# Hybrid block on one core: the low part of half of every second MLP weight tile made by an adding DMA, and 56 instead of 44 of the 128 pairs of K tiles by seven products

## The chip, the cores and the metric

The kernel runs on one core of one Trainium2 chip. The number that counts is the device time of one execution in microseconds, here the median of three runs. TensorE (PE in the profile) multiplies, VectorE (DVE), ScalarE (ACT) and GpSimd (POOL) work on tiles in the on-chip memory SBUF, PSUM holds the sums of TensorE, and SyncE (SP) issues most of the DMAs.

## The reference

One layer of a hybrid trunk on 256 tokens, width 2048, in float32. The change lies in the last third, the squared-ReLU MLP:

```python
D_MODEL = 2048; SEQ = 256; D_FF = 4 * D_MODEL
...
def squared_relu_mlp(n, w1, w2):
    return jnp.square(jax.nn.relu(n @ w1)) @ w2
...
    n = rms_norm(h, norm_mix_w[layer])
    h = h + hybrid_token_mixer(n, ...)      # input projection, two head groups, output projection
    n = rms_norm(h, norm_ffn_w[layer])
    h = h + squared_relu_mlp(n, w_ff1[layer], w_ff2[layer])
return rms_norm(h, norm_final_w)
```

`w_ff1` is 2048 x 8192 and `w_ff2` 8192 x 2048, so each is read once, as 64 tiles of 128 partitions x 2048 float32 (1 MB).

## The kernel before, in words

**Precision.** TensorE takes each float32 operand as two fp32r numbers: `hi`, the value rounded to fp32r, and `lo`, the rest. For a weight tile ACT makes `hi` by a copy (line 122) and DVE makes `lo = w - hi` (line 123). A product of two blocks is then three matmuls of 128x128 by 128x512: hi by hi, lo of the tokens by hi, hi of the tokens by lo of the weights (lines 925, 926, 927, in `product`).

**Pairs of K tiles.** A weight tile of the MLP holds a 2x2 block of the weight matrix: two blocks of the contraction dimension (a pair of K tiles) by two blocks of 512 columns, in the order B12, B11, B21, B22. The tokens come as a 2x2 block too (two halves of 128 tokens by the same two K tiles). Their product takes eight block products (`plain_quad`, 24 matmuls, summed in the four PSUM banks `E`), or seven with sums of blocks (Winograd's form of Strassen's scheme, `sum_quad`, 21 matmuls). The seven products need differences of the weight blocks, which DVE forms in `TT` (lines 965, 968, 969), and a third and half a fourth pair of hi and lo: `hi4`, `lo4`. They go into the first three banks of `E` and into four more banks `M`, which are joined once per column group (`joins`) and added to `E`.

**Which pairs.** `w_ff1` is worked in eight groups of 1024 columns (`ng`, lines 990 on), each over eight pairs `kp`; `SUMS` says which of them go by seven products: three in the even groups, four in the odd ones, 28 in all. The token operands (with their sums) are made once and stay in `sets` and `sets2`. `w_ff2` is worked in two halves (`q`, line 1105 on) of 32 pairs; `SUMS2` names eight of each 32, 16 in all. Its token operands are made pair by pair, `a2_plain` (one split of 512 columns, `gs`) or `a2_sums` (four sums `S` of 128 columns and splits of 384 and 512, `st`). Together 44 of 128 pairs go by seven products.

**Buffers.** Three buffers hold weight tiles (`wpool`). The pairs of hi and lo of 1024 columns go to five places in turn: three in `spool` (`hi`, `lo`) and two in `wp2` (`hi2`, `lo2`), in `split_pair`. `hi4`, `lo4`, `TT`, `S` and `st` have one place each.

**Order.** The program is written tile by tile, and a scheduler then sets the order on each engine; engines work in that order, and an instruction waits on its engine until what it needs is there and the place it writes is free. SP issues the loads of the weight tiles (lines 1000 and 1107), each once one of the three places is free. Between two groups of `w_ff1` the four finished outputs pass through ACT (relu), are transposed on PE (line 937) and squared by ACT (`turn`, line 939, held back in `fills`). POOL has no work in the MLP but two instructions at its end.

Of the kernel before, what the change touches and what calls it, by code (L numbers as in the profile page):

```python
# [75 lines left out]
def hybrid_block(ctx: ExitStack, tc: tile.TileContext, x, xt, w_in, w_ab, params, w_out, w_ff1, w_ff2,  # L76
# [747 lines left out]

    KP = KT // 2
    SUMS = ((2, 4, 6), (1, 2, 4, 6))
    WITH_SUMS = (2, 1, 4, 6)
    sets = bpool.tile([P, 8192], F32R, tag="xT", name="sets")  # L830
    sets2 = tp.tile([P, 3 * 1792], F32R, tag="s2", name="sets2")
    plain = [kp for kp in range(KP) if kp not in SUMS[0]]
# [4 lines left out]

    def a_sums(kp):
        n = WITH_SUMS.index(kp)
        t, at = (sets2, (n - 1) * 1792) if n else (sets, 6144)  # L840
        return t[:, at:at + 1792].rearrange("p (s n t) -> p s n t", s=2, n=7)

    h = hpool.tile([P, 2 * D], F32, tag="h", name="h").rearrange("p (f c) -> p f c", f=2)
# [68 lines left out]
    NF = DFF // P  # L912
    NG = NF // 2
    NGR = 8
    gt = []

    def g(kp):
# [33 lines left out]
            if (n, kk) == (3, 0):  # L951
                fill(n_fill)

    def plain_weights(w):
        B12, B11 = halves(split_pair(w[:, 0:1024]))
        B21, B22 = halves(split_pair(w[:, 1024:2048]))
        return (B11, B12), (B21, B22)

    def sum_quad(E, M, A, w, a0, z0):

        TT = tq.tile([P, 2048], F32, tag="TT", name="TT")
        B = [w[:, c * 512:(c + 1) * 512] for c in range(4)]
        T1, T2, T4 = [TT[:, c * 512:(c + 1) * 512] for c in (0, 2, 3)]
        B21, B22 = halves(split_pair(w[:, 1024:2048]))
        DVE.tensor_tensor(out=TT[:, 0:1024].rearrange("p (a c) -> p a c", a=2), in0=view(w, 0, [[1536, 2], [1, 512]]),
                          in1=view(w, 512, [[-512, 2], [1, 512]]), op=ALU.subtract)
        B1, B3 = halves(split_pair(TT[:, 0:1024]))
        DVE.tensor_tensor(out=T2, in0=B[3], in1=T1, op=ALU.subtract)
# [22 lines left out]
    for ng in range(NGR):  # L991


        bank_e, bank_m = (acc_a, acc_b) if ng % 2 == 0 else (acc_b, acc_a)
        E = [bank_e() for _ in range(4)]
        M = None
        with_sums = SUMS[ng % 2]
        for kp in range(KP):
            w = wtile()
            SP.dma_start(w, w_ff1[ng * KP + kp])  # L1000
            if kp not in with_sums:
                st = a_plain(kp)
                plain_quad(E, lambda kk, hf: [st[:, kk, c + hf * P:c + hf * P + P] for c in (0, T)], plain_weights(w),
                           kp == 0, kp == KP - 1, 0 if kp == 0 else 2)
                if kp == 0:
                    fill(4 if 1 in with_sums else 2)
                if ng == 0 and kp == 1:
                    for hf in range(2):
                        DVE.tensor_tensor(out=fs[:, 4 + hf:5 + hf], in0=fs[:, 2 * hf:2 * hf + 1],
                                          in1=fs[:, 2 * hf + 1:2 * hf + 2], op=ALU.add)  # L1010
                    DVE.tensor_scalar(fs[:, 4:6], fs[:, 4:6], 1.0 / D, EPS, ALU.mult, ALU.add)
                    DVE.reciprocal(fs[:, 6:8], fs[:, 4:6])
                    octx.close()
                    yctx.close()
                    fp = ctx.enter_context(tc.tile_pool(name="fp", bufs=1))
                    gt += [fp.tile([P, NG // 2, 4 * P], F32, tag=f"g{i}", name=f"g{i}") for i in range(2)]
                    cp = c1.enter_context(tc.tile_pool(name="cp", bufs=1))
                continue
            if M is None:
                M = [bank_m() for _ in range(4)]  # L1020
            st = a_sums(kp)
            sum_quad(E, M, [(st[:, 0, n, :], st[:, 1, n, :]) for n in range(7)], w, kp == with_sums[0],
                     kp == with_sums[-1])
            if kp == with_sums[-1]:
                C4 = joins(M)

        for at, p in ((0, E[0]), (2, E[1]), (1, E[2]), (3, E[3])):
            DVE.tensor_tensor(out=C4[:, at], in0=p, in1=C4[:, at], op=ALU.add)
            ACT.activation(C4[:, at], C4[:, at], AF.Relu)
            fills.append(lambda ng=ng, at=at, src=C4[:, at], acc=bank_e: turn(ng, at, src, acc))  # L1030
# [42 lines left out]
            DVE.tensor_scalar(h[:, hf, a:b], o[hf][:, a:b], s, None, ALU.mult)  # L1073
        (ACT if eng is ACT else SP).dma_start(out[0, hf * P:(hf + 1) * P, a:b], h[:, hf, a:b])

    SUMS2 = (3, 7, 10, 14, 17, 21, 24, 28)
    TAIL = 2
    KP2 = NF // 2

# [20 lines left out]
    for q in range(2):  # L1100
# [2 lines left out]
        M = None  # L1103
        held = []
        for kp in range(KP2):
            w = wtile()
            SP.dma_start(w, w_ff2[q * KP2 + kp])
            if kp in SUMS2:
                if M is None:
                    M = [bank_m() for _ in range(4)]  # L1110
# [123 lines left out]
```

## Time and profile before

| | |
|---|---|
| median of 3 runs | 1227.92 us (1227.33 to 1228.0) |
| the profiled execution, its own time | 1227.51 us |
| its span | 1225.8 us |
| mean granted TensorE clock | 0.997 |
| MLP in the profile | from 534 us to the end |

The span is what the profiler saw from the first to the last instruction; 1.71 us of the execution's own time lie around it. In the profile's groups a line can be that of a helper: line 123 is every subtraction that makes a `lo`, and the names before and after the arrow say of what.

### The profile page before, as it was taken

Reading aid. Unit: us, or ns where it says so; the run is one execution under the profiler, and the core shown is the slowest. Engines: PE = TensorE matmul, PEld = TensorE weight load, DVE = VectorE, ACT = ScalarE, POOL = GpSimd, SP = SyncE. Lnnn points to the kernel's source line nnn. Section 1 sums busy time; section 2 is a strip of 40 time slices with the busy share of each in tenths; the row PEclk is TensorE's granted clock in tenths of the full one; section 3 lists DMA queues with packets and bytes.
Section 4 is the critical chain, followed back from the end, with each engine's and each line's share of the span. In section 5 each row is a group of like instructions: output and inputs, shape, how many; then the busy total and the mean of one; then the engine's idle time right before and its main releaser. Section 6 shows DMA issues by size and latency. Waiting matters only on the chain.

```text
span 1225.8 us, 18164 instructions
## 1 busy us (share of the span) xinstructions
PE 1214.8 (99%) x6894; PEld 1007.3 (82%) x6894; DVE 1035.7 (84%) x1455; ACT 778.2 (63%) x1150; POOL 113.5 (9%) x165
## 2 busy tenths in 40 slices
PE   9999999999999999999999999999999999999997
PEld 7888888888778888888888888888888888888886
DVE  7878997799977886689889889889998888989887
ACT  7668766677756765565666656566676665656653
POOL 0132432135111110000000000000000000000000
PEclk9999999999999999999999999999999999999998
DMA  9455555555333555656455645654866556556461
GB/s 339 148 172 185 175 178 184 205 173 168 123 115 128 176 173 210 227 180 238 156 187 206 229 148 177 241 202 153 312 223 228 184 186 225 188 191 227 161 230 70
DMA packets 37144, 233.45 MB, mean 190 GB/s; under 512 B 4696, under 2 KB 5728, under 8 KB 10176
## 3 DMA queue, kind: packets, MB, share of 16 engines
q1 hardware_dynamic: 34848, 229.83, 53.5%
q0 software_dynamic: 1632, 1.72, 0.7%
q8 instruction: 54, 0.88, 0.3%
q10 hardware_dynamic: 576, 0.74, 0.2%
q14 instruction: 34, 0.28, 0.1%
HBM read 227.67 MB, written 4.60 MB: 189 GB/s over the span
## 4 chain that ended last, share of the span: by engine, by line
PE 98%; DMA 0%; issue 0%; DVE 0%; ACT 0%; SPq 0%; POOLq 0%; POOL 0%; DVEq 0%
PE acc L369 11%; PE acc L341 10%; PE acc L926 9%; PE acc L927 9%; PE acc L925 9%; PE accb L926 9%; PE accb L925 9%; PE accb L927 9%; PE acc L342 5%; PE acc L896 4%; PE accb L896 4%; PE accv L341 2%; PE accv L342 1%; PE accb L937 1%; PE acc L937 1%; PE pk L465 1%
## 5 line engine op out<-in xcount | busy, mean ns | idle before, releaser
L123 DVE TENSOR_TENSOR lo<-w,hi 128x1024 fp32r<-128x1024 f32 (+1 forms) x422 | 485.6, 1166 | 113.0 <-ACT hi L122 103.6
L122 ACT CAST hi<-w 128x1024 fp32r<-128x1024 f32 (+1 forms) x422 | 413.8, 994 | 233.1 <-PE acc L926 56.9
L341 PE MATMUL acc<-xT,hi 128*128 128x512 f32 x512 | 182.1, 401 | 1.5 <-ACT hi L122 1.5
L122 ACT CAST hi<-TT 128x1024 fp32r<-128x1024 f32 x88 | 92.0, 1052 | 77.5 <-issue 21.7
L342 PE MATMUL acc<-xT,lo 128*128 128x256 f32 x512 | 139.2, 284 | 0.0
L123 DVE TENSOR_TENSOR lo<-TT,hi 128x1024 fp32r<-128x1024 f32 x88 | 106.8, 1221 | 30.2 <-ACT hi L122 27.8
L369 PE MATMUL acc<-hi,xT 128*128 128x512 f32 x384 | 118.0, 395 | 0.0
L341 PEld LDWEIGHTS acc<-xT,hi 128*128 128x128 f32 x512 | 94.3, 188 | 21.1 <-ACT hi L122 2.0
L925 PE MATMUL acc<-hi,sets 128*128 128x512 f32 x260 | 101.4, 391 | 0.0
L926 PE MATMUL acc<-hi,sets 128*128 128x512 f32 x260 | 101.2, 390 | 0.0
L342 PEld LDWEIGHTS acc<-xT,lo 128*128 128x128 f32 x512 | 96.1, 189 | 4.9 <-DVE lo L123 1.2
L927 PE MATMUL acc<-lo,sets 128*128 128x512 f32 x260 | 95.9, 390 | 0.0
L925 PE MATMUL accb<-hi,sets 128*128 128x512 f32 x224 | 88.0, 393 | 0.0
L926 PE MATMUL accb<-hi,sets 128*128 128x512 f32 x224 | 87.3, 390 | 0.0
L369 PEld LDWEIGHTS acc<-hi,xT 128*128 128x128 f32 x384 | 70.4, 188 | 14.6
L927 PE MATMUL accb<-lo,sets 128*128 128x512 f32 x224 | 78.7, 391 | 0.0
L926 PE MATMUL acc<-hi,gs 128*128 128x512 f32 (+1 forms) x200 | 77.0, 385 | 0.0
L925 PE MATMUL acc<-hi,gs 128*128 128x512 f32 (+1 forms) x200 | 76.7, 385 | 0.0
L927 PE MATMUL acc<-lo,gs 128*128 128x512 f32 (+1 forms) x200 | 75.6, 385 | 0.0
L369 PE MATMUL acc<-lo,xT 128*128 128x512 f32 x192 | 73.2, 397 | 0.0
L926 PE MATMUL accb<-hi,gs 128*128 128x512 f32 x188 | 73.1, 389 | 0.0
L925 PE MATMUL accb<-hi,gs 128*128 128x512 f32 x188 | 72.6, 389 | 0.0
(367 smaller groups left out, 2279.2 us busy)
## 6 DMA issues: line engine op xcount, KB each, us to landing
w<-in_w_ff_dram SPq DMA_DIRECT2D x128, 1024.0 KB, 5.0
w<-in_w_in_dram SPq DMA_DIRECT2D x61, 1024.0 KB, 5.0
w<-in_w_out_dram SPq DMA_DIRECT2D x16, 1024.0 KB, 5.0
w<-in_w_in_dram SPq DMA_DIRECT2D x12, 256.0 KB, 5.4
big<-in_xt_dram SPq DMA_DIRECT2D x8, 256.0 KB, 5.8
h<-in_x_dram SPq DMA_DIRECT2D x2, 1024.0 KB, 6.1
scr_h<-h SPq DMA_DIRECT2D x4, 512.0 KB, 7.3
tail<-scr_h SPq DMA_DIRECT2D x2, 1024.0 KB, 8.5
```

The source lines that it names most:

```text
L122: ACT.copy(hi, w)
L123: last_lo[0] = eng.tensor_tensor(out=lo, in0=w, in1=hi.bitcast(F32), op=ALU.subtract)
L341: PE.matmul(accs[g], lhsT=hi[:, kk, g, :], rhs=xT[:, k, :], start=(k == 0), stop=False)
L342: mm = PE.matmul(accs[g][:, T:], lhsT=lo[:, kk, g, :], rhs=xT[:, k, 0:T], start=False, stop=(k == KT - 1))
L369: mm = PE.matmul(accs[hf], lhsT=xT[:, k, a + hf * P:a + hf * P + P], rhs=ww[:, cs], start=(k == 0 and a == 0 and ww is hi), stop=(k == KT ...
L465: PE.matmul(pk0, lhsT=R[:, 1, 0:P], rhs=qk.rearrange("p a t -> p (a t)"), start=True, stop=True)
L896: PE.matmul(accs[2 * hf + c], lhsT=st, rhs=ww[:, c * 512:(c + 1) * 512], start=(k == 0 and a == 0 and ww is hi), stop=(k == 2 * NH - 1 and ...
L925: PE.matmul(dst, lhsT=ah, rhs=bh, start=start, stop=False)
L926: PE.matmul(dst, lhsT=al, rhs=bh, start=False, stop=False)
L927: PE.matmul(dst, lhsT=ah, rhs=bl, start=False, stop=stop)
L937: PE.transpose(pt[:, c * P:(c + 1) * P], src[:, c * P:(c + 1) * P], ident)
```

## The change

In the MLP the tiles are now fetched by `ff_ahead`, which `ff_tile` calls two tiles ahead of the tile that is worked on. Of every second tile (the odd ones of 128) it also makes the low part of the second half (B21 and B22) without DVE: ACT writes the negated half to a new tile `lod` (as fp32r, so it is rounded as `hi` is), and POOL issues a DMA that reads the same half of the weights from HBM again and adds it to `lod`, so that w - hi stands there. `second_half` then makes only `hi` of that half, by ACT. `lod` has two places in `wp2`, 4 KB per partition each; the space that the program keeps for POOL's DMA descriptors is set to 8192 bytes per partition.

`SUMS` now names four pairs in the even groups and five in the odd ones (36 in all), `SUMS2` ten of each 32 (20 in all). Pair 1 is no longer plain in any group and pair 5 is plain in the even ones; the token sets are laid out anew for that, and the first group takes its pairs in the order 0, 3, 1, 5, 2, 4, 6, 7, with the weights laid out to match. From the second group on all four held-back `turn`s come after the first pair.

```diff
+    def ff_ahead(n):
+        while len(ff) <= min(n, 127):
+            i = len(ff)
+            src = w_ff1[i] if i < 64 else w_ff2[i - 64]
+            w, lo = wtile(), None
+            SP.dma_start(w, src)
+            if i % 2:
+                lo = wp2.tile([P, 1024], F32R, tag="lod", name="lod")
+                ACT.activation(lo, w[:, 1024:2048], AF.Copy, scale=-1.0)
+                POOL.dma_start(lo, src[:, 1024:2048], accum_op=ALU.add)
+            ff.append((w, lo))
+
+    def ff_tile(n):
+        ff_ahead(n + 2)
+        t, ff[n] = ff[n], None
+        return t
+
+    def second_half(wl):
+        w, lo = wl
+        if lo is None:
+            return split_pair(w[:, 1024:2048])
+        n = pairs[0] = pairs[0] + 1
+        pool, t = (spool, "") if n % 5 < 3 else (wp2, "2")
+        hi = pool.tile([P, 1024], F32R, tag="hi" + t, name="hi" + t)
+        ACT.copy(hi, w[:, 1024:2048])
+        return hi, lo
...
-    SUMS = ((2, 4, 6), (1, 2, 4, 6))
-    WITH_SUMS = (2, 1, 4, 6)
+    SUMS = ((1, 2, 4, 6), (1, 2, 4, 5, 6))
+    WITH_SUMS = (2, 5, 1, 4, 6)
...
-    def plain_weights(w):
-        B12, B11 = halves(split_pair(w[:, 0:1024]))
-        B21, B22 = halves(split_pair(w[:, 1024:2048]))
+    def plain_weights(wl):
+        B12, B11 = halves(split_pair(wl[0][:, 0:1024]))
+        B21, B22 = halves(second_half(wl))
...
-    def sum_quad(E, M, A, w, a0, z0):
+    def sum_quad(E, M, A, wl, a0, z0):
...
-        B21, B22 = halves(split_pair(w[:, 1024:2048]))
+        B21, B22 = halves(second_half(wl))
...
-        for kp in range(KP):
-            w = wtile()
-            SP.dma_start(w, w_ff1[ng * KP + kp])
+        for pos, kp in enumerate(ORDER[min(ng, 1)]):
+            w = ff_tile(ng * KP + pos)
...
-                           kp == 0, kp == KP - 1, 0 if kp == 0 else 2)
-                if kp == 0:
-                    fill(4 if 1 in with_sums else 2)
+                           pos == 0, pos == KP - 1, 2 if pos else 0)
+                if pos == 0:
+                    fill(4 if ng else 2)
...
-    SUMS2 = (3, 7, 10, 14, 17, 21, 24, 28)
+    SUMS2 = (2, 5, 8, 11, 14, 17, 20, 23, 26, 28)
...
-            w = wtile()
-            SP.dma_start(w, w_ff2[q * KP2 + kp])
+            w = ff_tile(64 + q * KP2 + kp)
...
+_ORDER = (0, 3, 1, 5, 2, 4, 6, 7)
...
-    nc = _bacc.Bacc("TRN2", target_bir_lowering=False, num_devices=1)
+    nc = _bacc.Bacc("TRN2", target_bir_lowering=False, num_devices=1, dynamic_dma_scratch_size=8192)
```

The scheduler places the new instructions. The first place is the passage from the sixth to the seventh group of `w_ff1` (tile 48 is the first and tile 49 the second of the new group). On ACT there stood before, from the casts of tile 47 (`w_7608`) on, with tile 48 `w_7654` and tile 49 `w_7700`:

```order
L122 CAST hi_7610<-w_7608 128x1024
L122 CAST hi2_7656<-w_7654 128x1024
L122 CAST hi_7660<-w_7654 128x1024
L983 COPY C4_7602<-acc_7360 128x512
L122 CAST hi_7702<-w_7700 128x1024
L122 CAST hi_7706<-w_7700 128x1024
L122 CAST hi4_7768<-w_7746 128x512
```

Now ACT has there (tile 48 is `w_7648`, tile 49 is `w_7697`, pair 1 of this group, which now goes by seven products):

```order
L122 CAST hi_7746<-w_7648 128x1024
L122 CAST hi_7750<-w_7648 128x1024
L1017 COPY C4_7691<-acc_7440 128x512
L837 ACTIVATE lod_7699<-w_7697 128x1024
L122 CAST hi4_7825<-w_7697 128x512
L853 CAST hi_7812<-w_7697 128x1024
L122 CAST hi2_7815<-TT_7811 128x1024
```

The negated copy stands right behind the copy of the finished bank `acc_7440`, which waits for PE, and the POOL DMA that adds to `lod_7699` waits for the negated copy. PE ends that bank with the row `acc_7440<-lo4_7667`; its rows up to the first use of `lod_7699` begin and end so:

```order
L960 MATMUL acc_7440<-lo4_7667,sets2_4888 128x512
L960 MATMUL accb_7373<-lod_7606,sets_4887 128x512
L960 MATMUL accb_7374<-lod_7606,sets_4887 128x512
L960 MATMUL accb_7376<-lod_7606,sets_4887 128x512
L960 MATMUL acc_7441<-lo_7657,sets2_4888 128x512
L960 MATMUL acc_7443<-lo_7657,sets2_4888 128x512
```

```order
L960 MATMUL acc_7741<-lo_7751,sets_4887 128x512
L958 MATMUL acc_7741<-hi_7812,sets2_4888 128x512
L959 MATMUL acc_7741<-hi_7812,sets2_4888 128x512
L960 MATMUL acc_7740<-lod_7699,sets2_4888 128x512
L960 MATMUL acc_7741<-lod_7699,sets2_4888 128x512
```

Between `acc_7440<-lo4_7667` and `acc_7740<-lod_7699` stand 33 matmuls of 128x512. Before, both halves of tile 49 came from lines 122 and 123, and PE waited there for no DMA.

The second place lies in `w_ff2`. Tile 79 (`w_9059`) is a plain pair behind tile 78 (`w_9022`), which goes by seven products. On ACT there stands now:

```order
L122 CAST hi4_9125<-w_9022 128x512
L122 CAST st_9104<-g0_5657 128x384
L122 CAST st_9104<-S_9099 128x512
L837 ACTIVATE lod_9061<-w_9059 128x1024
L122 CAST hi2_9115<-TT_9109 128x1024
L122 CAST hi_9121<-TT_9109 128x1024
```

`hi4` and `st` have one place each, so these casts wait until PE has read those of the pair by seven products before it (tile 75). The last such read on PE is the row `accb_8581<-lo4_8998`; its rows end at the first use of `lod_9061` so:

```order
L958 MATMUL acc_8479<-hi_9158,gs_9155 128x512
L959 MATMUL acc_8479<-hi_9158,gs_9155 128x512
L960 MATMUL acc_8479<-lo_9159,gs_9155 128x512
L958 MATMUL acc_8476<-hi_9162,gs_9155 128x512
L959 MATMUL acc_8476<-hi_9162,gs_9155 128x512
L960 MATMUL acc_8476<-lod_9061,gs_9155 128x512
```

Between `accb_8581<-lo4_8998` and `acc_8476<-lod_9061` stand 83 matmuls of 128x512. In all, PE has 4516 matmuls of 128x512 instead of 4552.

More of the change, by code (lines that the diff above doesn't have):

```diff
@@ L823, in split_pair @@
         return split(w, None, *[pool.tile([P, 1024], F32R, tag=p + t, name=p + t) for p in ("hi", "lo")])
+    ff = []
+    def ff_ahead(n):
[22 more added lines that the diff above has]
+        return hi, lo
     KP = KT // 2
-    SUMS = ((2, 4, 6), (1, 2, 4, 6))
-    WITH_SUMS = (2, 1, 4, 6)
+    SUMS = ((1, 2, 4, 6), (1, 2, 4, 5, 6))
+    WITH_SUMS = (2, 5, 1, 4, 6)
     sets = bpool.tile([P, 8192], F32R, tag="xT", name="sets")
@@ L839, in a_sums @@
         n = WITH_SUMS.index(kp)
-        t, at = (sets2, (n - 1) * 1792) if n else (sets, 6144)
+        t, at = (sets2, (n - 2) * 1792) if n > 1 else (sets, 4096 + n * 1792)
         return t[:, at:at + 1792].rearrange("p (s n t) -> p s n t", s=2, n=7)
@@ L914, in hybrid_block @@
     NGR = 8
+    ORDER = _ORDER, range(KP)
     gt = []
@@ L952, in plain_quad @@
                 fill(n_fill)
-    def plain_weights(w):
-        B12, B11 = halves(split_pair(w[:, 0:1024]))
-        B21, B22 = halves(split_pair(w[:, 1024:2048]))
+    def plain_weights(wl):
+        B12, B11 = halves(split_pair(wl[0][:, 0:1024]))
+        B21, B22 = halves(second_half(wl))
         return (B11, B12), (B21, B22)
-    def sum_quad(E, M, A, w, a0, z0):
+    def sum_quad(E, M, A, wl, a0, z0):
+        w = wl[0]
         TT = tq.tile([P, 2048], F32, tag="TT", name="TT")
@@ L1003, in hybrid_block @@
                 plain_quad(E, lambda kk, hf: [st[:, kk, c + hf * P:c + hf * P + P] for c in (0, T)], plain_weights(w),
-                           kp == 0, kp == KP - 1, 0 if kp == 0 else 2)
-                if kp == 0:
-                    fill(4 if 1 in with_sums else 2)
-                if ng == 0 and kp == 1:
+                           pos == 0, pos == KP - 1, 2 if pos else 0)
+                if pos == 0:
+                    fill(4 if ng else 2)
+                if ng == 0 and pos == 1:
                     for hf in range(2):
@@ L1192, in _laid_out @@
     f1 = i["w_ff1"][0].reshape(8, 2, P, 8, 2, 512)
+    f1 = np.stack([f1[list(_ORDER), :, :, 0]] + [f1[:, :, :, g] for g in range(1, 8)], 3)
     f2 = i["w_ff2"][0].reshape(32, 2, P, 2, 2, 512)
```

## The prediction

> **What bounds the kernel now.** First the page: busy shares and the chain that ended last.
>
> ```profile
> span 1225.8 us, 18164 instructions
> ...
> PE 1214.8 (99%) x6894; PEld 1007.3 (82%) x6894; DVE 1035.7 (84%) x1455; ACT 778.2 (63%) x1150; POOL 113.5 (9%) x165
> ...
> PE 98%; DMA 0%; issue 0%; DVE 0%; ACT 0%; SPq 0%; POOLq 0%; POOL 0%; DVEq 0%
> ```
>
> PE is busy from end to end and is the chain. A busy PE can still hide waits, so next the waits of PE over the whole span, and the stretches of the MLP:
>
> ```profile
> PE acc L341 <- ACT hi L122: 1.5, 2, 1.1
> PE warm L177 <- POOL pre L408: 1.0, 1, 1.0
> ...
> core 0: us, PE busy (x) PEld busy (x) DVE busy (x) ACT busy (x) POOL busy (x), PEclk, DMA share, GB/s
> 620.00:700.00 80.00, 80.00 (x370) 66.46 (x369) 71.38 (x79) 50.20 (x62) 0.00 (x0) 1.00 0.55 195
> 900.00:1000.00 100.00, 100.00 (x443) 82.81 (x442) 88.09 (x114) 61.17 (x75) 0.00 (x0) 1.00 0.59 207
> 1200.00:1226.00 26.00, 17.38 (x89) 14.68 (x87) 18.73 (x35) 7.51 (x16) 1.12 (x2) 0.88 0.22 82
> ```
>
> Both waits of PE lie in the input projection; in the MLP it never waits, at a granted clock of 1.00. So time goes only with matmuls, unless something new makes PE wait. Behind PE stands DVE at 88 to 89%, then ACT at 61 to 63%, and the DMA engines at 0.55 to 0.59. How far ACT and DVE run ahead shows in their own waits in the MLP (610 to 1200 us):
>
> ```profile
> DVE lo L123 <- ACT hi L122: 63.7, 59, 2.0
> ACT hi L122 <- PE acc L926: 61.2, 58, 3.8
> ACT hi L122 <- PE accb L926: 53.0, 46, 4.3
> ...
> ACT hi L122 <- DMA w<-in_w_ff_dram: 19.6, 17, 2.1
> ```
>
> ACT waits mostly for PE to free a place for `hi`: it is a full set of buffers ahead. It also stands 19.6 us before loads that are late, and none of that reaches PE.
>
> **The change part by part.**
>
> *Matmuls removed.* Matmuls overlap, so the price of one is the distance of two starts. 27 matmuls in a row on PE, the first and the last:
>
> ```profile
> 559.67 0.39 PE L925 MATMUL accb<-hi,sets 128*128 128x512 f32 x1
> ...
> 565.56 0.39 PE L927 MATMUL acc<-lo,sets 128*128 128x512 f32 x1
> ```
>
> (565.56 - 559.67) / 26 = 0.2265 us, not the 0.39 us of the row. Twelve more pairs by seven products drop 3 matmuls each: 36 x 0.2265 = **8.15 us** off the path, 5.4 in `w_ff1` (8 pairs) and 2.7 in `w_ff2` (4). The joins stay one per column group.
>
> *DVE and ACT.* Their rows, in the MLP from 640 us on:
>
> ```profile
> L123 DVE TENSOR_TENSOR lo<-w,hi 128x1024 fp32r<-128x1024 f32 x177 | 212.1, 1219 | 36.1 <-ACT hi L122 34.8 <-ACT C L983 0.5 <-PE acc L937 0.4
> L965 DVE TENSOR_TENSOR TT<-w 128x1024 f32<-128x1024 f32 x35 | 42.6, 1219 | 4.7 <-DMA w<-in_w_ff_dram 4.6
> L123 DVE TENSOR_TENSOR gs<-g,gs 128x512 fp32r<-128x512 f32 x48 | 32.7, 683 | 0.0
> L968 DVE TENSOR_TENSOR TT<-w,TT 128x512 f32<-128x512 f32 x35 | 23.9, 683 | 0.1
> L123 DVE TENSOR_TENSOR st<-g,st 128x384 fp32r<-128x384 f32 x16 | 8.8, 549 | 0.0
> L1087 DVE TENSOR_TENSOR S<-g 128x128 f32<-128x128 f32 x16 | 4.5, 282 | 0.0
> ...
> L122 ACT CAST hi<-w 128x1024 fp32r<-128x1024 f32 x176 | 183.6, 1053 | 93.1 <-PE acc L926 38.4 <-PE accb L926 36.4 <-issue 10.3
> L122 ACT CAST hi<-w 128x512 fp32r<-128x512 f32 x36 | 22.3, 620 | 24.2 <-DMA w<-in_w_ff_dram 14.1 <-PE acc L926 6.4 <-PE accb L926 3.8
> L122 ACT CAST gs<-g 128x512 fp32r<-128x512 f32 x48 | 29.4, 617 | 4.4 <-PE accb L927 2.5 <-PE acc L927 1.9
> L122 ACT CAST st<-g 128x384 fp32r<-128x384 f32 x16 | 8.2, 511 | 0.1
> L983 ACT COPY C<-acc 128x512 f32<-128x512 f32 x3 | 1.7, 577 | 0.0
> ```
>
> DVE loses 64 subtractions of 1219 ns, 78.0 us. A pair turned to seven products adds one more subtraction of 1024 columns (`TT` and its two `lo` for one `lo`: 3 - 1 = 2 of 1219 ns) and three of 683 ns: 4.49 us; in `w_ff2` also four `S` of 282, one of 683 and one of 549 for one `gs` of 683: 6.17 us. 8 x 4.49 + 4 x 6.17 = 60.6. DVE ends 17.4 us lower: it pays for the twelve pairs and stays under its 88%. ACT gains 64 negated copies, priced as the cast of the same shape at 1053 ns (67.4 us), and 1.67 us per new pair (1053 + 620; 2.19 in `w_ff2`, where 511 + 620 stand for 617): 22.1 us. 89.5 us more over the 640 us of the MLP lift ACT from 61% to 75%. Neither becomes the bound; beside PE both sums are hidden.
>
> *The adds.* 64 DMAs of 512 KB from POOL, whose queue is empty there. No adding DMA stands in this trace. The nearest rows are the loads of 1 MB from SP and the DMAs of 128 KB over 128 partitions from POOL in the mixer (first the median, then the eight DMAs' minimum, median and maximum, then one issue on POOL):
>
> ```profile
> w<-in_w_ff_dram SPq DMA_DIRECT2D x128, 1024.0 KB, 5.0
> ...
> dt<-scr_g POOLq DMA_DIRECT2D x8, 128.0 KB, 4.7
> ...
> DMA to landing us min/median/max: 3.2/4.7/5.7
> ...
> 103.22 0.57 POOL L453 DMA_DIRECT2D dt<-scr_g  x1
> ```
>
> 207 GB/s at a share of 0.59 are 351 GB/s for all engines, so 384 KB more cost 1.1 us: 4.7 + 1.1 = 5.8 us to landing, the lower end. If the destination has to be read as well, another 512 KB pass, 1.5 us: 7.3. I take the middle, 6.6, and keep both ends. In the Trainium skill, "DMA: Bandwidth & Descriptors", Anatomy of one DMA, a DMA from POOL costs 2.0 us and its bytes at 436 GB/s: an estimate of 3.2 us, with which nearly every add would be early and the time that of the rival in which all are hidden. For the 128 KB it gives 2.3 us, where the row has 4.7, so the row is taken.
>
> *What waits for an add.* The negated copy stands in ACT's queue, the casts of the next pairs behind it, and the matmul with `lod` in PE's. At the passage from the sixth to the seventh group ACT can copy `acc_7440` when PE is through with it; 33 matmuls later PE needs `lod_7699`. 33 x 0.2265 = 7.47 us, less 0.58 for the copy and 1.05 for the negated one, leave **5.8 us** for the add. In `w_ff2`, at tile 79, it is 83 x 0.2265 = 18.8 less 0.62 + 0.51 + 0.62 + 1.05: 16 us. Gone over in the same way, all 32 adds of `w_ff2` have 10 us or more, and in `w_ff1` seven have little: 5.8, 6.1, 6.5, 6.7, 6.8, 6.9 and 7.1, the others 7.8 and more. A landing of 6.6 us then costs 0.8 + 0.5 + 0.1 = **1.4 us** of PE, one of 5.8 nothing, one of 7.3 3.8 + 1.4 = 5.2 (1.5 + 1.2 + 0.8 + 0.6 + 0.5 + 0.4 + 0.2).
>
> *The loads beside them.* The adds take 1.5 us of all engines per two tiles (about 10.3 us at 22.7 matmuls a tile): the share of 0.59 becomes 0.74, or 0.88 with the destination read. A load that meets an add lands up to 1.5 us later. The negated copy, and all casts behind it, wait for that load, and the load waits for the last DVE reader of its place, as the queue of SP shows (`w_ff1`):
>
> ```profile
> SPq L1000 <- DVE lo L123: 200.7, 40, 16.6
> ```
>
> The eight passages between the groups of `w_ff1` (and into `w_ff2`) have the least cover. Between nothing, as before, and 8 x 1.5 = 12 us I take **2.5 us**: the 19.6 us that ACT waits now for loads without a mark on PE put it near the lower end.
>
> *The rest at nothing.* The new order of the first group, the token sets (two plain conversions fewer, one set of sums more) and the four `turn`s after the first pair lie beside PE's matmuls, as they already do in the odd groups, where PE has no wait; without that cover one set of sums is some 3 us, once. The smaller descriptor space could hold POOL's issues back (0.57 us now); each add is waited for before the next but one, so I see no reason. The last 26 us, where PE is busy 17.38, keep their work.
>
> *Sum.* -8.15 + 1.4 + 2.5 = -4.25: span 1225.8 - 4.25 = 1221.55, with the 1.71 us around it 1223.26. The profiled execution lies 0.41 us under the median (1227.51 and 1227.92), so the median comes to **1223.7 us**.
>
> **The rivals.**
>
> *All adds hidden.* For it: 16 us of cover in `w_ff2`. Against: 5.8 us at a place that needs 5.8 at best. 1227.92 - 8.15 = 1219.8 us.
>
> *Gain and waits cancel.* An add at the upper end (7.3 us): -8.15 + 5.2 + 2.5 = -0.45, and with loads 2 us worse +1.6: 1227 to 1230 us.
>
> *The add is slow (slower than before).* One mechanism: the add occupies the DMA engines about twice as long as a plain read of the same bytes and is met by loads, so it lands at 8.5 us or more, and PE waits in its queue at the `lod` matmuls of `w_ff1`. At 8.5 the shortfalls of the seven are 2.7 + 2.4 + 2.0 + 1.8 + 1.7 + 1.6 + 1.4 = 13.6, the next ones about 2: 15.5 + 2.5 - 8.15 = +9.9, 1237.8 us. It decides from the landing at which the shortfalls reach 8.15 - 2.5 = 5.65 us, about 7.4. For it: 5.7 us was already the longest landing of a quarter of the bytes. Against: the queue of POOL is free and ten microseconds stand before most adds. The Trainium skill bears on this case from the same page, Rules for kernel authors: an accumulating DMA reads its destination and writes it later. No run so far shows what that costs.
>
> *It doesn't do what it says* (DVE is not relieved because it waits for ACT's casts behind late negated copies): DVE's 63.7 us of waits for ACT already have cover, so this comes only together with the last one, and has its time.
>
> **How the numbers follow.** About 0.2%, 2.5 us, is what a measurement of this kernel can tell from no change: faster is below 1225.5, slower above 1230.4. The forecast (1221 to 1225.5) has 0.43, all adds hidden (1219.5 to 1221) 0.12, together faster 0.55. Cancelled 0.17. Slow adds 0.28. The range leaves out 0.03 below 1219.5 and 0.17 above 1238, where a landing over 8.5 us would take it; the forecast's own range is 1221 to 1225.5.
>
> **What would show it.** PE with 36 matmuls fewer at the same distance of starts; 64 rows of `lod` on ACT near 1.05 us; DVE's share not above 88%; the DMA share between 0.7 and 0.9. The landing of `lod` is the number to read first: up to 6.6 us bears the forecast out, over 7.4 the slow rival. The waits of PE should name `lod` DMAs and ACT's casts, in `w_ff1` alone, some 4 us in all. Waits of PE in `w_ff2`, or more than 8 us of them, would prove me wrong, as would a lower granted clock.

## The result, and the profile after

The changed kernel takes 1267.77 us (median of 4 runs, 1265.75 to 1269.16) against 1227.62 us of the kernel before, measured beside it. The ratio is 1.0326, with a 95% interval of 1.0308 to 1.0344: slower by 40 us, where 4 us faster was forecast and the range ended at 1238. First the page of the changed kernel, busy shares and the chain that ended last:

```profile
span 1266.9 us, 18307 instructions
...
PE 1224.7 (97%) x6858; PEld 1002.9 (79%) x6858; DVE 1021.2 (81%) x1474; ACT 848.7 (67%) x1243; POOL 169.8 (13%) x229
...
PE 65%; DMA 12%; issue 10%; DVE 8%; ACT 4%; POOL 1%; POOLq 0%; SPq 0%; DVEq 0%; ACTq 0%
```

PE was 98% of the chain, and is 65% now. The chain goes through DMAs (12%), and DVE and ACT, all of which had lain beside PE. The idle time of PE rose from 1225.8 - 1214.8 = 11.0 to 42.2 us, and it is busy 9.9 us longer although 36 matmuls are gone. Where it waits in the MLP (534 to 1240 us; total, times, longest):

```profile
PE accb L960 <- DMA lod<-in_w_ff_dram: 8.2, 3, 3.6
PE acc L960 <- DMA lod<-in_w_ff_dram: 5.8, 5, 2.0
PE acc L958 <- ACT hi L122: 4.9, 6, 2.0
PE accb L960 <- DVE lo L123: 4.8, 3, 2.8
PE acc L960 <- DVE lo L123: 3.0, 5, 1.8
```

It waits 14.0 us for adds (`lod`), all of them in `w_ff1`, and 12.7 us in these rows for ordinary casts and subtractions. In `w_ff2` its waits are for DVE's low parts (7.2 us) and a join (1.5 us) alone. What holds these is in the waits of ACT and DVE in the same stretch:

```profile
ACT lod L837 <- DMA w<-in_w_ff_dram: 145.7, 50, 6.6
...
DVE TT L999 <- DMA w<-in_w_ff_dram: 43.1, 15, 4.3
...
ACT hi L122 <- PE acc L959: 16.4, 13, 3.5
```

In the kernel before, ACT's waits in the same stretch were:

```profile
ACT hi L122 <- PE acc L926: 71.8, 69, 3.8
ACT hi L122 <- PE accb L926: 56.3, 52, 4.3
...
ACT hi L122 <- DMA w<-in_w_ff_dram: 22.5, 19, 2.5
```

There ACT stood 128 us waiting for PE to free a place, so it was a full set of buffers ahead, and 22.5 us waiting for loads. Now it stands 146 us with the negated copy at the head of its queue, waiting for the load of the weight tile. It is hardly ahead any more. The queues and landings (packets, MB, share of 16 engines; then KB and median us from issue to landing):

```profile
q1 hardware_dynamic: 34848, 229.83, 50.8%
q0 software_dynamic: 10848, 35.27, 16.0%
...
w<-in_w_ff_dram SPq DMA_DIRECT2D x128, 1024.0 KB, 6.8
...
lod<-in_w_ff_dram POOLq DMA_DIRECT2D x64, 512.0 KB, 6.3
```

The adds land in 6.3 us, better than the 6.6 forecast. The loads, which did not change, land in 6.8 instead of 5.0. Of the kernel before the same row read:

```profile
q0 software_dynamic: 1632, 1.72, 0.7%
```

That is 8.6 us of 1225.8; so an add of 512 KB takes (16.0% x 1266.9 - 8.6) / 64 = 3.0 us of all sixteen engines. Two stretches show what is left of PE, and the engines at 0.79 and 0.90 where 0.55 and 0.59 stood:

```profile
core 0: us, PE busy (x) PEld busy (x) DVE busy (x) ACT busy (x) POOL busy (x), PEclk, DMA share, GB/s
...
700.00:800.00 100.00, 96.03 (x430) 77.00 (x429) 82.91 (x94) 67.82 (x82) 7.54 (x10) 1.00 0.79 230
...
900.00:1000.00 100.00, 98.45 (x442) 81.27 (x442) 82.01 (x119) 70.69 (x92) 8.00 (x10) 1.00 0.90 286
```

The first of them in the kernel before (the second stands in the prediction):

```profile
700.00:800.00 100.00, 100.00 (x460) 82.97 (x460) 88.00 (x100) 59.22 (x74) 0.00 (x0) 1.00 0.55 198
```

For the comparisons below each MLP stage gets one length: `w_ff1` from the first matmul with `sets` to the first with `gs`, `w_ff2` from there to the end of the span. In the changed kernel these are the rows (duration minimum, median, maximum; first and last start):

```profile
L958 PE MATMUL acc<-hi,sets x14: 389/389/477, 534.3 to 544.9; 128*128 128x512 f32 x14
...
L958 PE MATMUL acc<-hi,gs x54: 388/389/478, 905.8 to 959.8; 128*128 128x512 f32 x54
```

So `w_ff1` takes 371.5 us and `w_ff2` 361.1, where the kernel before has 343.8 and 347.9: 27.7 and 13.2 us more. All runs, with the lengths from the same rows of theirs:

| kernel | median us | ratio to before, 95% | w_ff1 | w_ff2 | load / add landing |
|---|---|---|---|---|---|
| before | 1227.6 | | 343.8 | 347.9 | 5.0 / - |
| changed | 1267.8 | 1.0326 [1.0308, 1.0344] | 371.5 | 361.1 | 6.8 / 6.3 |
| thin44 | 1227.8 | 1.0004 [0.9994, 1.0013] | 343.7 | 347.9 | 5.0 / 2.9 |
| thin_add | 1228.9 | 1.0011 [0.9998, 1.0024] | 346.0 | 345.6 | 5.0 / 3.8 |
| adds44 | 1256.1 | 1.0231 [1.0201, 1.0260] | 361.5 | 358.6 | 7.1 / 7.2 |
| traffic | 1232.7 | 1.0053 [1.0018, 1.0087] | 347.9 | 350.1 | 6.9 / 7.5 |
| plain_read | 1249.8 | 1.0182 [1.0119, 1.0246] | 353.6 | 357.0 | 6.4 / 4.9 |
| half_add | 1258.2 | 1.0251 [1.0221, 1.0281] | 362.8 | 360.6 | 6.7 / 5.0 |
| pairs56 | 1248.0 | 1.0165 [1.0135, 1.0194] | 365.3 | 346.0 | 4.9 / - |
| adds_f2 | 1237.6 | 1.0070 [1.0047, 1.0094] | 345.1 | 358.5 | 5.9 / 5.9 |
| pairs48 | 1226.7 | 0.9991 [0.9983, 1.0000] | 344.4 | 346.6 | 5.0 / - |
| four_w | 1260.3 | 1.0268 [1.0250, 1.0285] | 378.5 | 349.2 | 7.1 / 8.1 |
| four_thin | 1233.0 | 1.0045 [1.0028, 1.0062] | 348.0 | 348.1 | 5.1 / 4.0 |
| four_skip | 1248.0 | 1.0165 [1.0146, 1.0184] | 366.0 | 347.3 | 6.2 / 7.7 |
| half_first | 1278.4 | 1.0413 [1.0391, 1.0435] | 379.0 | 367.9 | 6.9 / 7.3 |
| neg_pool | 1291.9 | 1.0523 [1.0492, 1.0553] | 380.1 | 375.8 | 7.0 / 6.4 |
| lo_pool | 1307.9 | 1.0656 [1.0625, 1.0687] | 391.9 | 379.9 | 5.1 / - |

The loads of `half_first` in the last column are those of whole tiles. The lengths come from one profiled execution of each kernel. The runs of one kernel lie up to 6.6 us apart (of the eight runs of `traffic`, seven lie between 1229.6 and 1234.9 us and one at 1245.5), so a difference of 2 or 3 us between two lengths shows little.

### The profile page after: what moved, and what is told of

The parts are those of the page before. It is cut to its first block, busy times and chain, and to the rows that moved or that the text cites. A ratio compares the mean times of both kernels' runs of the same rounds, so it can differ in the third digit from the quotient of the medians.

```text
span 1266.9 us, 18307 instructions
## 1 busy us (share of the span) xinstructions
PE 1224.7 (97%) x6858; PEld 1002.9 (79%) x6858; DVE 1021.2 (81%) x1474; ACT 848.7 (67%) x1243; POOL 169.8 (13%) x229
## 4 chain that ended last, share of the span: by engine, by line
PE 65%; DMA 12%; issue 10%; DVE 8%; ACT 4%; POOL 1%; POOLq 0%; SPq 0%; DVEq 0%; ACTq 0%
PE acc L369 10%; PE acc L341 9%; DMA w<-in_w_ff_dram 9%; PE acc L342 5%; DVE lo L123 5%; PE accb L960 4%; PE accb L959 4%; PE accb L958 4%; PE acc L960 4%; PE acc L959 4%; PE acc L958 4%; PE acc L927 3%; PE accb L927 3%; DMA lod<-in_w_ff_dram 3%; PE accv L341 2%
## 5 line engine op out<-in xcount | busy, mean ns | idle before, releaser
L123 DVE TENSOR_TENSOR lo<-w,hi 128x1024 fp32r<-128x1024 f32 (+1 forms) x358 | 403.6, 1139 | 103.2 <-ACT hi L122 89.4
L122 ACT CAST hi<-w 128x1024 fp32r<-128x1024 f32 (+1 forms) x358 | 340.7, 965 | 115.9 <-PE acc L369 21.7
L123 DVE TENSOR_TENSOR lo<-TT,hi 128x1024 fp32r<-128x1024 f32 x112 | 135.6, 1220 | 45.8 <-ACT hi L122 42.0
L837 ACT ACTIVATE lod<-w 128x1024 fp32r<-128x1024 f32 x64 | 67.9, 1061 | 154.3 <-DMA w<-in_w_ff_dram 150.0
L838 POOL DMA_DIRECT2D lod<-in_w_ff_dram x64 | 56.0, 875 | 721.4 <-ACT lod L837 501.0
L122 ACT CAST hi<-TT 128x1024 fp32r<-128x1024 f32 x112 | 116.0, 1046 | 34.2 <-DVE TT L1003 12.9
L999 DVE TENSOR_TENSOR TT<-w 128x1024 f32<-128x1024 f32 x56 | 68.4, 1221 | 43.7 <-DMA w<-in_w_ff_dram 43.1
L960 PE MATMUL acc<-lo,sets 128*128 128x512 f32 x200 | 71.7, 394 | 0.6 <-DVE lo L123 0.6
L959 PE MATMUL acc<-hi,gs 128*128 128x512 f32 (+1 forms) x184 | 70.7, 385 | 0.0
L958 PE MATMUL acc<-hi,gs 128*128 128x512 f32 (+1 forms) x184 | 70.7, 386 | 0.0
L853 ACT CAST hi<-w 128x1024 fp32r<-128x1024 f32 x64 | 67.0, 1048 | 5.4 <-PE acc L959 2.7
```

The source lines that it names most:

```text
L122: ACT.copy(hi, w)
L123: last_lo[0] = eng.tensor_tensor(out=lo, in0=w, in1=hi.bitcast(F32), op=ALU.subtract)
L837: ACT.activation(lo, w[:, 1024:2048], AF.Copy, scale=-1.0)
L853: ACT.copy(hi, w[:, 1024:2048])
L958: PE.matmul(dst, lhsT=ah, rhs=bh, start=start, stop=False)
L959: PE.matmul(dst, lhsT=al, rhs=bh, start=False, stop=False)
```

## The experiments

### Pairs, adds and traffic taken apart

`adds44` keeps the adds and goes back to the 44 pairs of the kernel before (and to its order):

```diff
-    SUMS = ((1, 2, 4, 6), (1, 2, 4, 5, 6))
+    SUMS = ((2, 4, 6), (1, 2, 4, 6))
-    SUMS2 = (2, 5, 8, 11, 14, 17, 20, 23, 26, 28)
+    SUMS2 = (3, 7, 10, 14, 17, 21, 24, 28)
```

> The adding DMAs alone: the 44 pairs by seven products of the kernel before, in their old order, but the low part of half of every second MLP tile made by the negated copy and the add. Theory A (late loads: the adds make the weight loads land later, 6.8 instead of 5.0 us, and the negated copy holds ACT's queue until its tile has landed): nearly the whole loss stays, 1260 to 1276 us, with ACT waiting 100 us or more ahead of the negated copies. Theory B (late adds: PE waits for the low part itself): also 1255 to 1276, but with the PE waits named after the add. Theory C (the twelve more pairs crowd DVE and ACT): 1227 to 1232 us, since the pairs are the old ones.

`pairs56` has the 56 pairs and no add (`if i % 2 and False:`), so DVE makes every low part:

> The twelve more pairs alone: 56 pairs by seven products, every low part by DVE as before, no add. DVE carries 60.6 us more than before, from 88 to about 98% in the MLP. Theories A and B: no late loads and no late adds, so between 1219.8 (all hidden) and 1236 us (DVE bound in the denser groups), weight loads at 5.0 us. Theory C: most of the loss, 1250 us or more.

`thin_add` lets the adding DMA carry 64 of 1024 columns; all else is the changed kernel, and the rest of the low part is left out:

```diff
-                POOL.dma_start(lo, src[:, 1024:2048], accum_op=ALU.add)
+                POOL.dma_start(lo[:, 0:64], src[:, 1024:1088], accum_op=ALU.add)
```

> The changed kernel with an add of 64 instead of 1024 columns, so 2 instead of 32 MB; the order, the negated copies and every wait stay. The output leaves out the low part of the other 960 columns of these halves. Theory A: the weight loads land in 5.0 to 5.3 us again, ACT's wait ahead of the negated copies falls under 50 us, and the time falls to 1220 to 1228 us. If instead the order of the queues were the cause, whatever the traffic: 1250 us or more with loads at 5.0.

`thin44` is `adds44` with the thin add:

> 44 pairs as before, the low part by the negated copy and an add of 64 columns (the other 960 columns of the low part are left out): all of the change but its pairs and its traffic. The thin add on 56 pairs took 346.0 us in w_ff1 where 343.8 - 5.4 = 338.4 were to be had. If the 7.6 us lie in the eight further pairs of w_ff1 (their sums at the passages): w_ff1 344 here, 1227 to 1229. If they lie in the negated copies at the head of ACT's queue: w_ff1 348 to 352, 1232 to 1237.

The waits of ACT before the negated copy and of PE for `lod`, of `adds44`:

```profile
ACT lod L837 <- DMA w<-in_w_ff_dram: 125.4, 55, 5.1
```

```profile
PE accb L960 <- DMA lod<-in_w_ff_dram: 11.9, 5, 5.0
```

and ACT's line of `thin44`, with a stretch of `w_ff1` in which PE has no gap:

```profile
ACT lod L837 <- DMA w<-in_w_ff_dram: 28.5, 24, 3.1
```

```profile
700.00:800.00 100.00, 100.00 (x460) 83.04 (x459) 78.83 (x90) 68.50 (x83) 8.74 (x10) 1.00 0.62 208
```

With 44 pairs the 64 negated copies, the 64 issues on POOL and the waits for (small) adds cost nothing: 343.7 and 347.9 us, as before. Put the full adds in, and 17.8 + 10.7 = 28.5 us come on top. With 56 pairs the full adds cost 371.5 - 346.0 = 25.5 and 361.1 - 345.6 = 15.5, together 41.0 us. So the bytes of the adds are the loss, and not the order or ACT's new work alone. Against the expectations: `adds44` (1256.1) lies 4 us under theory A and at the low end of B; `pairs56` (1248.0) lies between the 1236 us of A and B and the 1250 of C; `thin_add` (1228.9, and 50.4 us of ACT's waits) is just over A's bounds; `thin44` is as its first case said.

The pairs paid less than their matmuls. From `thin44` to `thin_add` `w_ff2` falls by 2.3 us (2.7 were counted), but `w_ff1` rises by 2.3 where it should fall by 5.4: 7.7 us are lost there without any traffic to speak of. In `thin_add` PE waits 4.2 us in the MLP, for casts, low parts, a join and (0.7 us) an add; what takes the rest was not found. The gain in `w_ff2` is no surer: `four_thin` below has the same pairs and 348.1 us there. In `pairs56` `w_ff1` takes 365.3 us with DVE at 87% of the span:

```profile
PE 1218.0 (98%) x6858; PEld 997.0 (80%) x6858; DVE 1089.0 (87%) x1538; ACT 798.7 (64%) x1179; POOL 113.9 (9%) x165
```

Relief for DVE is therefore worth 365.3 - 346.0 = 19.3 us in `w_ff1` with 36 pairs, and 0.4 in `w_ff2` with 20.

### Late loads, or late adds

Two theories were open. A: the adds make the loads late, and these hold ACT's queue. B: the adds themselves land too late for PE. `plain_read` makes each add a plain DMA of the same bytes (the whole half then stands in place of its low part); `half_add` adds 512 columns only (the low part of the others is left out); `traffic` is the kernel before with 64 adds of 512 KB into two spare tiles that nothing reads, each issued when the load of its tile has landed:

```diff
# plain_read
-                POOL.dma_start(lo, src[:, 1024:2048], accum_op=ALU.add)
+                POOL.dma_start(lo, src[:, 1024:2048])
# half_add
+                POOL.dma_start(lo[:, 0:512], src[:, 1024:1536], accum_op=ALU.add)
# traffic, against the kernel before
+            t = spares[n // 2 % 2]
+            POOL.tensor_copy(t[:, 0:1], w[:, 0:1])
+            POOL.dma_start(t, src[:, 1024:2048], accum_op=ALU.add)
```

> The changed kernel with the 64 adds turned into plain DMAs of the same bytes to the same place (the output leaves out the subtraction: the whole half stands where its low part should). The bytes moved, the order and all waits stay. In the changed kernel the adds take 16.0 - 0.7% of 16 engines' time, 3.0 us each, where a load of 1 MB takes 2.9 us: twice the price per byte. Theory A1 (the time that the adds occupy on the engines delays the loads): 1.5 us each, 8% of the engines, loads at 5.5 to 6.3 us, 1233 to 1250 us. Theory A2 (reading the weights a second time from HBM delays the loads, whether they are added or not): 1260 to 1268 us.

> The changed kernel with adds of 512 instead of 1024 columns (the output leaves out the low part of the other 512 columns). Half the bytes, each at the price of an add, so about the same time on the engines as the plain DMAs of all 1024 columns: 1.5 us each. Theory A1: within 5 us of that kernel. Theory A2: half way between the kernel with adds of 64 columns (1229) and the changed one (1268), near 1248, whatever the other does.

> The kernel before (44 pairs, every low part by DVE, no negated copy) with 64 adds of 512 KB into two spare tiles that nothing reads, each issued by POOL when the weight tile of its turn has landed. Nothing waits for the adds. Theory A with the loads alone as the cause (the adds delay the loads, and three places for weight tiles don't cover it): loads at 6.5 us or more and 1240 to 1260 us. If the loss needs the negated copy in ACT's queue or a low part that comes late: 1227 to 1232 us, with loads as late.

First POOL's queue, the loads and ACT's and PE's waits of `plain_read`:

```profile
q0 software_dynamic: 10848, 35.27, 9.0%
...
w<-in_w_ff_dram SPq DMA_DIRECT2D x128, 1024.0 KB, 6.4
...
ACT lod L837 <- DMA w<-in_w_ff_dram: 125.7, 48, 5.9
...
PE accb L960 <- DMA lod<-in_w_ff_dram: 0.3, 1, 0.3
```

The queue of `half_add`, then of `traffic` ACT's waits for loads and for PE:

```profile
q0 software_dynamic: 10848, 18.50, 8.8%
```

```profile
ACT hi L122 <- DMA w<-in_w_ff_dram: 69.2, 30, 6.2
ACT hi L122 <- PE acc L936: 52.8, 55, 2.9
```

The same bytes as a plain read take (9.0% x 1244.8 - 8.6) / 64 = 1.6 us of the engines, half of the add's 3.0; half the bytes as an add take (8.8% x 1257.7 - 8.6) / 64 = 1.6 too. An add occupies the engines as long as twice its bytes read plainly. In `plain_read` PE waits 0.6 us in all for `lod`, yet the MLP is 7.6 + 11.4 = 19.0 us longer than with the thin add: loads that land at 6.4 us do that without any late add. That speaks for A. So does `w_ff2`, which is 13.2 us longer than before in the changed kernel and 10.7 in `adds44`, where none and 0.2 us of PE's waits name an add. It does not come from lateness alone: in `traffic` the loads are as late as in the changed kernel (6.9), and the two stages lose only 4.1 + 2.2 = 6.3 us. There ACT waits for loads too, but half as long, and still has waits for PE in between, so it catches up. Late loads cost little beside the old work, the negated copies cost nothing beside punctual loads, and both together (`adds44`) cost 28 us with the same pairs, 11.9 of them waits of PE for adds.

The time on the engines is not shown to be the whole price. `plain_read` lies at the upper end of what A1 allowed, with its two runs 6.5 us apart. `half_add`, with the same time on the engines, is 8.4 us slower, where A1 allowed 5 and A2 put it near 1248. The intervals of the two overlap, so this stays open.

### More room for the loads

`four_w` gives the weight tiles four places instead of three; the space comes from the descriptor space and a junk output that now goes to tile `S`:

```diff
-    wpool = ctx.enter_context(tc.tile_pool(name="wpool", bufs=3))
+    wpool = ctx.enter_context(tc.tile_pool(name="wpool", bufs=4))
-    nc = _bacc.Bacc("TRN2", target_bir_lowering=False, num_devices=1, dynamic_dma_scratch_size=8192)
+    nc = _bacc.Bacc("TRN2", target_bir_lowering=False, num_devices=1, dynamic_dma_scratch_size=3072)
```

> The changed kernel with four places for weight tiles instead of three (the space comes from a smaller descriptor space, 3072 bytes per partition, and from a junk output put into the tile S). The engines carry the same loads and adds, but SP may issue each load when a fourth place is free, about one tile (10 us) earlier. Theory A (the adds make the loads late by about 1.8 us, and the late loads hold ACT's queue, and only then PE): with 10 us more of cover the waits of ACT for loads fall from some 144 us to under 50, as in the run with the thin add, and the time comes to 1220 to 1232. Theory B (the adds themselves land too late for PE, whatever the loads do): 1255 to 1268, since the adds start no earlier than the negated copies let them. Theory C (the DMA engines are simply full in places): the loads stay at 6.8 us, ACT still waits, 1255 or more.

```profile
ACT lod L837 <- DMA w<-in_w_ff_dram: 22.6, 15, 4.2
...
PEld acc L960 <- DMA lod<-in_w_ff_dram: 9.2, 2, 4.9
PE acc L960 <- DMA lod<-in_w_ff_dram: 8.4, 2, 4.5
```

ACT's waits before the negated copies fell from 146 to 22.6 us, as A said, and `w_ff2` from 361.1 to 349.2: there A holds. But `w_ff1` grew to 378.5, and the time came to 1260 where A had promised 1232 at most. (The expectation counted 10 us for the fourth place; a tile takes 691.7 / 128 = 5.4 us of the MLP before.) The adds now land at 8.1 us in the median for 6.3, and that they meet loads that are issued earlier is argued from that, not shown. PE's waits for adds in `w_ff1` did not grow, 12.3 us for 14.0; its idle time there rose by 4 us, and the clock fell (first the changed kernel, then `four_w`, each over its `w_ff1`):

```profile
534.30:905.80 371.50, 350.54 (x1557) 282.60 (x1556) 304.97 (x359) 253.63 (x314) 27.93 (x32) 0.99 0.75 225
```

```profile
534.30:912.80 378.50, 353.23 (x1558) 288.05 (x1556) 306.86 (x358) 255.25 (x314) 27.10 (x31) 0.96 0.73 220
```

With a granted clock of 0.96 for 0.99, about 0.04 x 378.5 = 15 us go to the lower clock where 0.01 x 371.5 = 4 went before, an estimate from these two rows. The section on the hardware comes back to it. `four_thin` and `four_skip` ask for what holds `w_ff1`. The first puts the thin add into `four_w`; the second leaves out the add of the first odd tile of each group of `w_ff1` (DVE makes that low part):

```diff
-            if i % 2:
+            if i % 2 and (i >= 64 or i % 8 != 1):
```

> The kernel with four places for weight tiles and an add of 64 columns only (the low part of the other 960 columns is left out). It has the order and the places without the traffic. If the traffic of the adds is what holds w_ff1 with four places: 1220 to 1229, w_ff1 338 to 347. If the order with four places holds it by itself: w_ff1 360 or more, 1245 or more.

> The kernel with four places for weight tiles, and in w_ff1 no add for the first odd tile of each group (eight of 32; DVE makes the low part of these). With four places w_ff2 took 349.2 us from its first matmul to the end (361.1 with three, 347.9 before) but w_ff1 378.5 (371.5 with three, 343.8 before). Theory: w_ff1 is held at the passages between the groups, where SP issues up to four loads at once and the add of the first odd tile lands 10 to 12 us late among them; without these eight adds w_ff1 falls to 350 to 360 and the time to 1232 to 1242. Rival: the adds stall PE anywhere in a group of w_ff1, and the next one takes their place: w_ff1 at 370 or more, 1252 to 1262.

`four_thin`: 348.0 us in `w_ff1`, so the traffic holds it with four places too; its time, 1233.0, is 4 us over what was expected. `four_skip`: 366.0 us, neither the 350 to 360 of the theory nor the 370 of its rival. Its chain between 540 and 890 us, the shares by line:

```profile
by line: DMA w<-in_w_ff_dram 15.5%; PE acc L958 10.7%; PE acc L960 10.5%; PE acc L959 10.5%; PE accb L958 9.1%; PE accb L959 9.0%; PE accb L960 8.7%; issue 8.4%; DVE lo L123 5.7%; ACT hi L122 2.8%; PE accb L970 1.8%; ACT C L1062 1.1%; DVE T
```

PE's waits for `lod` are 1.2 us now, so leaving out the adds at the passages was worth 12.5 us, but late loads stand on the chain in their place. In `w_ff1` both theories hold in part.

`half_first` cuts the load of every second tile in two, the half that the negated copy reads first:

```diff
+                SP.dma_start(w[:, 1024:2048], src[:, 1024:2048])
+                SP.dma_start(w[:, 0:1024], src[:, 0:1024])
```

> The changed kernel with the load of every second tile cut in two DMAs of 512 KB, the half that the negated copy reads first. Theory A says that the negated copy stands at the head of ACT's queue before a late load: it would then wait only for the first half, 1.5 to 2.5 us less for each of some 49 waits, and 10 to 25 us of the loss come back: 1243 to 1258. If all casts are late, and not the negated copy in particular, the casts of the other half wait instead and the time stays at 1262 to 1270.

It got worse by 10.6 us. ACT's waits for loads fell only to 116 us, and DVE's for the other half rose from 43.1 to 57.8 (line 1003 is its `TT`):

```profile
ACT lod L841 <- DMA w<-in_w_ff_dram: 116.2, 50, 5.5
...
DVE TT L1003 <- DMA w<-in_w_ff_dram: 57.8, 21, 5.2
```

That is worse than either case allowed. Splitting also adds 64 DMAs, so the run does not settle how much hangs on the negated copy itself; it gives no sign that this copy in particular needs the load early.

`adds_f2` has adds in `w_ff2` alone, with 20 pairs there, and `w_ff1` of the kernel before:

```diff
-            if i % 2:
+            if i % 2 and i >= 64:
-    SUMS = ((1, 2, 4, 6), (1, 2, 4, 5, 6))
+    SUMS = ((2, 4, 6), (1, 2, 4, 6))
```

> Adds in w_ff2 alone, with 20 pairs by seven products there; w_ff1 has no add and the 28 pairs of the kernel before, in its old order. 12 matmuls fewer are worth 2.7 us. If the 13.2 us by which w_ff2 grew in the changed kernel arise there from its own late loads: 1238 to 1243. If w_ff2 only inherits arrears from w_ff1 (its adds had 10 us and more of cover in the prediction): 1223 to 1228.

`w_ff2` takes 358.5 us, 10.6 more than before: so most of its loss arises there and is not inherited, though PE waits for no `lod`.

### Other ways to relieve DVE, and the pairs alone

`neg_pool` lets POOL make the negated copy, `lo_pool` lets POOL subtract the low part with no add at all:

```diff
# neg_pool
-                ACT.activation(lo, w[:, 1024:2048], AF.Copy, scale=-1.0)
+                POOL.tensor_scalar(lo, w[:, 1024:2048], -1.0, None, ALU.mult)
# lo_pool, in second_half
+        POOL.tensor_tensor(out=lo, in0=w[:, 1024:2048], in1=hi.bitcast(F32), op=ALU.subtract)
```

> The changed kernel with the negated copy made by POOL instead of ACT, so that the wait for a late load holds only POOL's queue, where nothing else stands; ACT has 68 us less to do. The adds and their bytes stay. Theory A: ACT's casts no longer wait behind late tiles, the time falls to 1225 to 1245 us, though the loads still land late. Theory B: the low part comes as late or later (POOL's copy is slower), PE's waits for the add grow, 1265 us or more. Theory C: no change, 1262 to 1270.

> A candidate: the changed kernel's 56 pairs, with the low part of the same 64 halves subtracted by POOL from the tile and its high part, and no negated copy and no add. POOL's copy of the shape took 3.3 us and lengthened DVE's 128x1024 subtraction from 1.22 to 1.29 us, so DVE's 1024 us become some 1060 and POOL has 64 x 3.3 = 211 us or more. If late loads were the cause of the loss: loads at 5.0 us, and 1220 to 1235 us. If POOL's share of DVE's time weighs more: 1235 to 1250 us.

```profile
L837 POOL TENSOR_SCALAR lod<-w 128x1024 fp32r<-128x1024 f32 x64 | 212.1, 3314 | 510.6 <-DMA w<-in_w_ff_dram 380.8
```

```profile
L852 POOL TENSOR_TENSOR lod<-w,hi 128x1024 fp32r<-128x1024 f32 x64 | 179.9, 2811 | 640.1 <-ACT hi L851 594.4
...
L998 DVE TENSOR_TENSOR TT<-w 128x1024 f32<-128x1024 f32 x56 | 80.8, 1443 | 32.6 <-DMA w<-in_w_ff_dram 32.3
```

Both are far worse. POOL takes 3.3 and 2.8 us for what ACT does in 1.06 and DVE in 1.22, and DVE's subtraction into `TT` is slower beside it: 1290 ns in `neg_pool`, 1443 in `lo_pool`, for 1221. `neg_pool` takes the negated copies out of ACT's queue and is no test of that queue alone, since the slower copy makes the adds late: PE waits 28.8 us for them (534 to 1240 us). In `lo_pool` the loads land in 5.1 us and there is no add; PE waits 30.6 us for DVE's low parts instead.

`pairs48` is the kernel before with the new `SUMS2`, 48 pairs and no add:

> The kernel before with ten instead of eight pairs of each 32 of w_ff2 by seven products, 48 in all, and no add: 12 matmuls fewer, DVE 4 x 6.17 = 25 us more within the 348 us of w_ff2 (88% to some 92% at most, 95% if all of it falls on its tight stretches). If DVE still has room: 1227.4 - 2.7 = 1224.7. If DVE becomes the bound there, as it did with 56 pairs (20.6 us over before): 1228 to 1234.

```profile
1000.00:1100.00 100.00, 100.00 (x443) 82.84 (x442) 94.96 (x126) 63.59 (x84) 0.00 (x0) 1.00 0.56 197
```

DVE is at 95% and PE still has no gap. Its ratio, 0.9991 [0.9983, 1.0000], is 1 us, within the 0.2% that can't be told from no change; of the 2.7 us counted, `w_ff2` in the profile fell by 1.3. No kernel here is clearly better than the one before.

## Why the prediction was wrong, point by point

**Matmuls removed (-8.15).** They are gone, and where PE does not stall, its starts still lie 0.227 us apart. Without the traffic (`thin44` to `thin_add`) the twelve in `w_ff2` brought 2.3 of 2.7 us; the 24 in `w_ff1` brought nothing.

**DVE and ACT (hidden).** Durations and sums were near: the negated copy 1061 ns for 1053, DVE 14.5 us lower for 17.4. That they are hidden beside PE holds without the adds' traffic for 44 pairs (`thin44`); for 56 it holds less well, as the 7.7 us lost in `w_ff1` show. It missed that ACT's place ahead of PE is the cover for late loads.

**The adds (6.6 us to landing).** Measured 6.3: right. But the cost to others was taken as 1.5 us of the engines per add, with 3.0 as the other case. It is 3.0.

**What waits for an add (+1.4).** 14.0 us. The landings lie between 5.5 and 11.2 us, and the median of 6.3 hides the passages. At the first one PE waited so for the add of a copy at 575.77 (start, duration, the wait before it and its releaser in brackets; the first row is SP's queue, five loads issued over 16.78 us):

```profile
566.15 16.78 SPq L834 DMA_DIRECT2D w<-in_w_ff_dram  x5
...
575.77 1.06 ACT L837 ACTIVATE lod<-w 128x1024 fp32r<-128x1024 f32 x1
...
577.12 0.87 POOL L838 DMA_DIRECT2D lod<-in_w_ff_dram  x1 [11.39 <-ACT lod L837]
...
585.07 0.73 PE L960 MATMUL accb<-lod,sets 128*128 128x512 f32 x2 [2.25 <-DMA lod<-in_w_ff_dram]
```

From 577.12 to 585.07 the add took 7.9 us, beside loads that SP issued in the same microseconds. Here the add meets the loads just where the cover is least.

**The loads beside them (+2.5).** This is the step that failed. It had the right mechanism, adds that delay loads and casts that queue behind a waiting copy, but the size was taken from the 19.6 us that ACT waited without a mark on PE. Loads land 1.8 us later in the median, ACT waits 146 us for them, and its reserve is used up. Both terms together were 3.9 us; the runs with full and thin adds differ by 41.0. Of these 14.0 are PE's waits for adds, so 27.0 (the lower clock included) are left for a term that stood at 2.5; 15.5 of them lie in `w_ff2`, where no wait of PE names an add.

**The sum.** 41.0 for the traffic, 7.7 for the pairs of `w_ff1`, 0.4 for those of `w_ff2`, less the 3.9 allowed: 45.2, against 1266.9 - 1221.55 = 45.35 between the two spans.

**The rivals.** The slow add came nearest: the engines are occupied twice as long, as it said, and the outcome is on its side. But it priced only the `lod` matmuls (1237.8) and let the landing decide, from 7.4 us on. The landing stayed at 6.3, so the sign that was to bear the forecast out was seen, and the forecast was wrong. The sign to read was the landing of the loads. PE waits in `w_ff2`, more than 8 us of waits and a lower clock, the three things that were to prove it wrong, all came.

## What to carry to other kernels

Price a new DMA by what it takes from the transfers that are already there: read the share of the engines, and ask how far ahead of the bound engine each reader of the delayed loads runs. An idle wait that costs nothing today is a reserve, and work added to that engine's queue spends it. Change one of the two at a time (the copies without the bytes, the bytes without the copies), since each alone cost at most 6.3 us here.

## What the runs showed of the hardware

**The adding DMA.** 3.0 us of the sixteen engines for 512 KB, 1.6 for 256 KB, against 1.6 for 512 KB read plainly. The adds, on POOL's queue, delay loads on SP's from 5.0 to 6.8 us. The Trainium skill, "DMA: Bandwidth & Descriptors", Queues, rings and completion order, says that each engine takes packets in turn from the queues that have work; the later loads fit that, but no run here shows the turns themselves.

**A stall can cost again in the clock.** After the wait of 2.25 us shown above PE's next matmuls, in the changed kernel, and the granted clock of four microseconds (PEclk, the third number from the end):

```profile
586.95 0.63 PE L958 MATMUL accb<-hi,sets 128*128 128x512 f32 x1
587.38 0.63 PE L959 MATMUL accb<-hi,sets 128*128 128x512 f32 x1
587.80 0.63 PE L960 MATMUL accb<-lo,sets 128*128 128x512 f32 x1
...
586.00:590.00 4.00, 4.00 (x15) 3.19 (x14) 2.78 (x4) 2.25 (x4) 0.00 (x0) 0.57 0.96 222
```

Starts lie 0.43 us apart instead of 0.227 for some 3.4 us, and the clock is 0.57. In the MLP of the changed kernel four such stretches follow its four longest pauses, 2.5 to 4.0 us between two starts; after its pauses of up to 2.4 us the clock stays full. The length alone does not decide: in `half_add` the clock stays full after pauses of 2.7 and 3.1 us and halves after one of 1.4. Over the span the mean granted clock is 0.991 for 0.997 before, an estimated 0.006 x 1266.9 = 7.6 us; in `four_w`, with stalls of up to 6 us, it is 0.984, about 16 us. The Trainium skill, "TensorE: Matmul & The Clock Gate", Part 1, gives 426.7 ns between cold matmuls of this width, after an idle window of about 3.4 us. The distance agrees; three of the four pauses in the changed kernel were shorter.

**POOL beside DVE.** POOL's work on whole tiles lengthened DVE's subtraction of 1024 columns into `TT` from 1221 to 1290 ns (`neg_pool`) and 1443 ns (`lo_pool`) in the mean. The median stays at 1224 ns in both; single ones take up to 2.06 and 3.43 us.
